# Attention values, projections and window scores in full 128x128 products, in a two-layer hybrid trunk on one core

## The chip, the cores and the metric

The kernel runs on 1 core of one Trainium2 chip. The metric is the device time of one execution in microseconds (us); three runs of the kernel before are known, and one profiled execution of it. Engines are named as in the profile: PE (TensorE matmul), PEld (its weight loads), DVE (VectorE), ACT (ScalarE), POOL (GpSimd), SP (the queue that issues the loads).

## The reference, cut to what matters

512 latent tokens and 256 context tokens, 1024 features, go through two layers. A layer is: half a SwiGLU, a mixer with four parallel parts, half a SwiGLU. In the last layer only the 512 latent tokens are wanted of the mixer's output. The part of the mixer that the change touches is the two attentions:

```python
q_a = mla_q(z_lat[0], g_mla_q, w_mla_uq, tab)      # 4 heads, 64 plain + 32 rotary
k_a, v_a = mla_kv(z_lat[1], z_lat[2], g_mla_kv, w_mla_ukv, tab)
o_a = dense_attend_blocked(q_a, concat(k_a, kc_a), concat(v_a, vc_a))   # latent queries: 768 keys
o_c = window_attend_latent(q, k, v, k_ctx, v_ctx, sink)  # 4 query heads, 2 key heads, 64 wide
# softmax in both; context queries attend to the 256 context tokens only
```

The query latent has 192 features (128 + 64), the key and value latent 128.

## The kernel before, in words

All activations lie with features on partitions and tokens along the free dimension. Every float32 operand is split into two parts of 12 bits, x = hi + lo (`split`, lines 128 to 134: ACT copies hi, DVE subtracts to get lo), and a product is three passes on PE (`mm3`, L162): lo\*hi, hi\*lo, hi\*hi; a pass over 768 tokens is two instructions, of 512 and 256 columns. The instruction order on each engine is fixed at build time by a scheduler that goes by program order, with `rise(n)` for work to be taken n instructions earlier.

`mixer(l, n, st)` runs once a layer, with n = 768 tokens in the first layer and 512 in the second (nq = 6 or 4 blocks of 128). It makes the modulated norm `x` (16 tiles), the input projection tile by tile (`proj`), the key and value latent `mkv`, the query latent `mqa` (128 rows) and `mqb` (its other 64 rows, split into two tiles; the 64 rows below are free), the window's `wq`, `wk`, `wv`, and the short convolution. Then comes attention, as a pipeline over units:

- `Latent(h, tp)`: 256 queries of a head; 4 heads by 3 or 2 units. `softmax` makes scores (three passes of 96 rows, L162), a maximum (L852), the exponential (L855) and a normalisation on POOL (L857).
- `Window(t, kv)`: 128 queries, one key head, two query heads (`g`). `softmax` makes the scores of the local blocks (L793), adds a mask by a product (L796), and the scores of the context blocks (L798). Each score is two passes: one with a head's hi and lo part stacked to 128 rows, one with hi alone, 64 rows.
- `turned` transposes the weights in blocks of 128 (L595) and splits them; `values` multiplies them with V in the one PSUM bank `po` (the tile `pone`): `mm3` with 64 columns of V's hi or lo part as the loaded operand and 256 columns of transposed softmax weights moving, three instructions for each key block. One ACT copy takes the result out: L879 (latent), L832 (window).

In step i the loop emits the scores of unit i, the transposes of unit i-1 and the values of unit i-2. `first_head` runs inside the short convolution, before the last of its column tiles (`pb`): weights, head 0, and the scores of unit 0. `mla_head` makes a head: `mla_rotary` for each pair of heads (64 columns), 64 columns of plain queries, 64 columns of keys; heads 1 to 3 are made at steps 1, 4, 7 (first layer) or 1, 3, 5 (second). `mla_query` is six passes: three with the 128 rows of `mqa`, three with the 64 rows of `mqb`. PSUM pieces: two double banks `dbls` (scores, projections), and two single banks `sgl` (transposes, V), which take the place of a third double bank once `pb` has been read.

Of the kernel before, what the change touches and what calls it, by code (L numbers as in the profile page):

```python
# [46 lines left out]
class K:  # L47
# [4 lines left out]
    LAGS, HEAD = (1, 2), 1  # L52
# [4 lines left out]
    def __init__(self, tc, ctx, a, out):  # L57
# [7 lines left out]
        # PSUM: two banks, and six that each phase cuts for itself  # L65
# [8 lines left out]
    # ---- buffers: handed out and given back in program order  # L74
# [5 lines left out]
    def area(self, name, side="left"):  # L80
        """A phase's buffers: each in a pool of its own, so that it waits only for the users of its own bytes."""
# [37 lines left out]
    def rise(self, n):  # L119
        """Work that the scheduler is to take as if it came n instructions earlier."""  # L120
# [6 lines left out]
    # ---- exact two-part split: x = hi + lo, each of 12 significant bits  # L127
# [13 lines left out]
    def unit(self, src, neg=False):  # L141
        """A split [parts, <= 512] block of weights."""
# [12 lines left out]
    def mm3(self, ps, w, x, start, stop):  # L155
        """ps += w^T x for split operands, each [K, M] / [K, N]; N is cut at PSUM's banks."""
# [49 lines left out]
    def need(self, l, part):  # L206
        """Has what is left of a part of the modulation computed."""
# [7 lines left out]
    def norm_gain(self, l, part, ks=(0, 4)):  # L215
        """g * (1 + scale), both conditions."""
# [32 lines left out]
    def sums(self, ps, tiles, n):  # L249
        """The sum over partitions and tiles, on all partitions."""  # L250
# [6 lines left out]
    def rsqrt(self, out, x, scale):  # L257
        """1 / sqrt(scale * x + eps)"""
# [3 lines left out]
    def spread(self, ps, rc):  # L262
        """A row of values by token on all partitions, from columns of values by token."""
# [3 lines left out]
    def inv_rms(self, ps, tiles, n, scale, j0=0):  # L267
        """1 / sqrt(scale * sum of squares + eps) on all partitions (in PSUM), found by token."""
# [9 lines left out]
    def rnorm(self, a, b, ps=None):  # L278
        """1 / rms(h) for tokens [a, b), on all partitions (in PSUM)."""
# [3 lines left out]
    def modulated(self, hi, lo, t, k, r, gain, l, part, a, b):  # L283
        """hi + lo = h[k] * gain * r + shift for tokens [a, b)."""
# [25 lines left out]
    def token_sums(self, X, hn):  # L310
        """T1 = B12 - B11, T2 = B22 - T1, T3 = B22 - B12, T4 = T2 - B21, split."""
# [24 lines left out]
    def half_load(self, idx, rs, f, m, kk):  # L336
        """Half of the features of the gate's (m = 0) or the up product's (m = 1) column tile f."""
# [8 lines left out]
    def whole(self, ps, w, x, hn, start, stop):  # L346
        """ps += a whole product over half of the features."""
# [4 lines left out]
    def hidden(self, g, j, hn, pss):  # L352
        """silu(gate) * up, split, for half j of the tokens."""
# [8 lines left out]
    def plain(self, idx, f, X, g, hn, fills):  # L362
        """The split hidden tile f by plain products."""
# [11 lines left out]
    def first_pairs(self, idx, X, g, hn, norm, operands, fills, start):  # L375
        """The first four hidden tiles by plain products, while the operands are being made."""
# [47 lines left out]
    def gate_up(self, idx, f, X, g, hn, fills):  # L424
        """g[0], g[1]: the split hidden tiles f and f + 1."""
# [192 lines left out]
    def mixer(self, l, n, st):  # L618
# [353 lines left out]
        for i in range(2):  # L972
# [9 lines left out]
            if i == 1:  # L982
                first_head()
# [306 lines left out]
```

## Time and profile before

| what | value |
|---|---|
| median of 3 runs | 2734.28 us (2730.88 to 2735.37) |
| span of the profiled execution | 2729.7 us, 41155 instructions |
| PE busy | 2687.2 us, 98% (16292 matmuls) |
| PEld busy | 2458.7 us, 90% |
| DVE busy | 1998.7 us, 73% |
| ACT busy | 1108.8 us, 41% |
| POOL busy | 65.5 us, 2% |
| mean granted TensorE clock | 0.995 |

The span runs from the first to the last instruction; of the profiled execution no other time is given, and its span lies 4.6 us below the median of the runs. A matmul's time in the profile reaches from its start to the end of its passage, so that neighbours overlap: what one costs in a stream is the distance from its start to the next one's start.

### The profile page before, as it was taken

The page shows a single profiled execution, that of the slowest core. Times are in us where ns is not written, and L with a number is a line of the kernel's source. Part 1 is how long each engine was busy: PE and PEld are TensorE (multiplying, and loading weights), DVE is VectorE, ACT ScalarE, POOL GpSimd, SP SyncE. Part 2 cuts the span into 40 slices and gives each one's busy share as a digit, 9 for nine tenths or more (in the row PEclk, how much of TensorE's full clock was granted, in tenths as well). Part 3 has the DMA queues.
Part 4 walks back from the last instruction along what each step waited for, and adds up shares of the span by engine and source line. Part 5 has one row for each costly group of instructions (what it writes and reads, how often), then busy time and mean ns, then how long its engine had stood idle before and what let it go on. Part 6 is the DMA issues. An engine that isn't in the chain of part 4 may idle for free.

```text
span 2729.7 us, 41155 instructions
## 1 busy us (share of the span) xinstructions
PE 2687.2 (98%) x16292; PEld 2458.7 (90%) x16292; DVE 1998.7 (73%) x3884; ACT 1108.8 (41%) x2096; POOL 65.5 (2%) x88
## 2 busy tenths in 40 slices
PE   7999999999999999999999999999999999999998
PEld 5999999988876899999999999999998877899998
DVE  5777666779785476767667867776678785698887
ACT  4333323343375342333234523343244375444444
POOL 0000000000022000000000000000000021000000
PEclk9999999999999999999999999999999999999999
DMA  7323222321123342323223132222222122423322
GB/s 269 108 101 100 79 96 90 108 83 57 55 78 93 109 139 93 101 93 103 83 85 124 48 100 70 63 79 60 63 85 99 58 78 78 138 94 98 104 93 78
DMA packets 78241, 254.83 MB, mean 93 GB/s; under 512 B 8672, under 2 KB 14048, under 8 KB 77792
## 3 DMA queue, kind: packets, MB, share of 16 engines
q1 hardware_dynamic: 78048, 252.21, 28.7%
q8 instruction: 127, 2.08, 0.3%
q14 instruction: 66, 0.54, 0.1%
HBM read 250.08 MB, written 2.10 MB: 92 GB/s over the span
## 4 chain that ended last, share of the span: by engine, by line
PE 94%; DVE 4%; DMA 1%; ACT 1%; issue 1%; POOL 0%; DVEq 0%; SPq 0%; POOLq 0%; ACTq 0%
PE ps L162 73%; PE pone L162 10%; PE pmod L179 3%; PE pmod L162 3%; PE ps L595 1%; PE ps L793 1%; PE ps L798 1%; DVE r L134 0%; DMA raw<-in_w_gu 0%; DVE sm L852 0%; PE ps L796 0%; DMA mraw<-in_w_mod 0%; DVE wl L134 0%; PE ps L272 0%; PE pone L272 0%
## 5 line engine op out<-in xcount | busy, mean ns | idle before, releaser
L162 PE MATMUL ps<-x,wh 128*128 128x384 f32 (+1 forms) x3064 | 748.9, 329 | 0.0
L162 PEld LDWEIGHTS ps<-x,wh 128*128 128x128 f32 x3064 | 542.7, 188 | 0.1
L162 PE MATMUL ps<-x,wl 128*128 128x384 f32 (+1 forms) x1532 | 506.1, 331 | 0.0
L133 ACT ACTIVATE wh<-raw 128x512 fp32r<-128x512 f32 (+1 forms) x445 | 278.3, 626 | 486.9 <-PE ps L162 336.3
L134 DVE TENSOR_TENSOR wl<-raw,wh 128x512 fp32r<-128x512 f32 (+1 forms) x445 | 305.2, 687 | 121.9 <-ACT wh L133 119.1
L162 PE MATMUL ps<-t,wh 128*128 128x384 f32 (+2 forms) x1488 | 385.2, 341 | 0.3 <-DVE t L134 0.3
L162 PE MATMUL ps<-r,wh 128*128 128x512 f32 (+7 forms) x1432 | 355.5, 350 | 0.3 <-DVE r L291 0.3
L296 DVE SCALAR_TENSOR_TENSOR h<-ps,hg,h 128x256 f32<-128x256 f32 (+3 forms) x404 | 186.8, 506 | 186.6 <-PE ps L162 186.1
L162 PEld LDWEIGHTS ps<-x,wl 128*128 128x128 f32 x1532 | 287.6, 188 | 12.9 <-issue 10.7
L162 PEld LDWEIGHTS ps<-t,wh 128*128 128x128 f32 x1488 | 269.2, 188 | 7.2 <-DVE t L134 0.5
L133 ACT ACTIVATE wh<-t 128x512 fp32r<-128x512 f32 x217 | 136.0, 629 | 337.1 <-PE ps L162 201.9
L162 PEld LDWEIGHTS ps<-r,wh 128*128 128x128 f32 (+3 forms) x1432 | 236.4, 184 | 36.1 <-DVE r L291 1.5
L450 DVE TENSOR_TENSOR t<-t,ps 128x384 f32<-128x384 f32 (+1 forms) x422 | 217.2, 520 | 52.6 <-PE ps L162 50.2
L162 PE MATMUL ps<-t,wl 128*128 128x384 f32 (+2 forms) x744 | 253.4, 342 | 1.6 <-ACT t L133 1.6
L162 PE MATMUL ps<-r,wl 128*128 128x512 f32 (+5 forms) x716 | 225.1, 355 | 2.4 <-ACT r L290 1.3
L134 DVE TENSOR_TENSOR wl<-t,wh 128x512 fp32r<-128x512 f32 x217 | 149.1, 689 | 95.2 <-ACT wh L133 95.0
L133 ACT ACTIVATE t<-t 128x384 fp32r<-128x384 f32 (+2 forms) x247 | 130.2, 536 | 208.9 <-DVE t L444 100.7
L162 PE MATMUL ps<-x,t 128*128 128x384 f32 (+1 forms) x1308 | 204.4, 310 | 0.0
L162 PEld LDWEIGHTS ps<-x,t 128*128 128x128 f32 x1308 | 194.4, 188 | 0.0
L162 PE MATMUL ps<-t,t 128*128 128x384 f32 (+2 forms) x948 | 188.9, 345 | 0.0
L162 PEld LDWEIGHTS ps<-t,t 128*128 128x128 f32 x948 | 165.5, 188 | 10.9 <-issue 1.2
L134 DVE TENSOR_TENSOR t<-t,t 128x384 fp32r<-128x384 f32 (+2 forms) x247 | 137.4, 568 | 25.4 <-ACT t L133 25.0
(215 smaller groups left out, 3711.0 us busy)
## 6 DMA issues: line engine op xcount, KB each, us to landing
raw<-in_w_gu SPq DMA_DIRECT2D x160, 512.0 KB, 3.8
mraw<-in_w_mod SPq DMA_DIRECT2D x128, 512.0 KB, 4.0
raw<-in_w_dn SPq DMA_DIRECT2D x88, 512.0 KB, 3.7
raw<-in_w_in SPq DMA_DIRECT2D x34, 512.0 KB, 3.3
raw<-in_w_out SPq DMA_DIRECT2D x20, 512.0 KB, 3.4
i<-in_w_mod SPq DMA_DIRECT2D x32, 256.0 KB, 6.0
raw<-in_w_gu SPq DMA_DIRECT2D x32, 256.0 KB, 3.5
h<-in_h SPq DMA_DIRECT2D x4, 768.0 KB, 6.6
```

What stands on the lines that cost most here:

```text
L133: self.nc.scalar.activation(hi, x, AF.Copy)
L134: self.nc.vector.tensor_tensor(out=lo, in0=x, in1=hi.bitcast(F32), op=ALU.subtract)
L162: self.nc.tensor.matmul(ps[:, c:e], a, b[:, c:e], start=start and i == 0, stop=stop and i == 2)
L179: nc.tensor.matmul(ps[32 * j:32 * j + 32, :256], self.sc[:, k, :], r[:, j * 256:(j + 1) * 256], start=k == 0, stop=k == KD - 1)
L296: nc.vector.scalar_tensor_tensor(out=self.h[:, k, s:e], in0=ps[:, s - a:e - a], scalar=gate[:, k, i:i + 1], in1=self.h[:, k, s:e], op0=ALU ...
L450: eng.tensor_tensor(out=out, in0=p, in1=q, op=op)
L595: self.nc.tensor.transpose(out, in_, self.ident)
L793: nc.tensor.matmul(ps[:, c0:SEQ], a, b[:, kc], start=i == 0, stop=False)
L798: nc.tensor.matmul(ps[:, SEQ:TOK], a, b[:, SEQ:], start=i == 0, stop=i == 1)
```

## The change

- V's hi and lo parts of a head lie side by side in 128 columns (`value_blocks`); `weigh` multiplies them with the lo and then the hi part of the weights, two instructions for each key block; the result's two halves of 64 rows are summed by an ACT copy and a DVE addition (`summed`).
- Queries and keys of the latent attention are projected for two heads at a time (128 columns): `mla_queries`, `mla_keys`; the rotary parts of all four heads at once (`mla_rotary`). `mqb` is one tile with hi in the lower and lo in the upper 64 rows; its weights (`query_weights`) are stacked both ways, so that the second part of `mla_query` is two passes of 128 rows in place of three of 64.
- Both passes of the window's scores have 128 rows (`wks` holds two stacked tiles for each key head).
- Order: only the queries of heads 0 and 1 are made before `pb`; their keys, the V tiles and the scores of unit 0 come after it; the pair 2, 3 is made at step 4 (first layer) or 2 (second).

```diff
-    LAGS, HEAD = (1, 2), 1
+    LAGS, PAIR = (1, 2), {3: 4, 2: 2}
...
+        def value_blocks(ts, src):
+            for j, t in enumerate(ts):
+                v = t.rearrange("p (q c d) -> p q c d", c=2, d=64)
+                self.split(v[:, :, 0, :], v[:, :, 1, :], src[:, j * 384:(j + 1) * 384].rearrange("p (q d) -> p q d", d=64))
+        def weigh(t, b, p, start, stop):
+            v = t[:, b * P:(b + 1) * P]
+            nc.tensor.matmul(po[:, :256], v, p[1], start=start, stop=False)
+            nc.tensor.matmul(po[:, :256], v, p[0], start=False, stop=stop)
+        def summed(out, c, w):
+            nc.scalar.activation(out, po[64:, c:c + w], AF.Copy)
+            nc.vector.tensor_tensor(out=out, in0=po[:64, c:c + w], in1=out, op=ALU.add)
...
-                    parts = (q[:, ts_], wks[1 + kv]), (q[rows, ts_], wks[0][rows])
+                    parts = (q[:, ts_], wks[kv][0]), (q[:, ts_], wks[kv][1])
...
-                    self.mm3(po[:64], (wvs[0][:, d], wvs[1][:, d]), p, j == 0, j == len(w.kts) - 1)
+                    weigh(wvs[kt // 3], kt % 3 * 2 + w.kv, p, j == 0, j == len(w.kts) - 1)
...
-                    nc.scalar.activation(oc[w.kv][...], po[:64, g * P:(g + 1) * P], AF.Copy)
+                    summed(oc[w.kv][...], g * P, P)
...
-                    self.mm3(po[:64], (vh[:, d], vl[:, d]), p, kt == k0, kt == 5)
+                    weigh(vt[b // 6], b % 6, p, kt == k0, kt == 5)
...
+        def mla_query(ps, c, wa, wb):
+            self.mm3(ps, (wa[0][:, c:c + P], wa[1][:, c:c + P]), (mqa[0][:, :n], mqa[1][:, :n]), True, False)
+            for i, w in enumerate(wb):
+                for a in range(0, n, 512):
+                    e = min(n, a + 512)
+                    nc.tensor.matmul(ps[:, a:e], w[:, c:c + P], mqb[:, a:e], start=False, stop=i == 1)
+        def mla_rotary(wa, wb):
+            ps, q = self.turn(self.dbl), self.S()
+            mla_query(ps[:, :n], 256, wa, wb)
+            nc.scalar.activation(q[:, :n], ps[:, :n], AF.Copy)
+            self.rope(q, 0, P, self.cos_m, self.sin_m, self.mask_m)
+            rot.extend(self.split_new(q[:, :n], n))
...
+        def mla_keys(h, w):
+            ps = self.turn(self.dbl)
+            self.mm3(ps, (w[0][:, h * 64:h * 64 + P], w[1][:, h * 64:h * 64 + P]), mkv, True, True)
+            for u in range(2):
+                kh, kl = ks[h + u] = self.R(), self.R()
+                self.split(kh[:64, :], kl[:64, :], ps[u * 64:u * 64 + 64, :TOK])
...
         def mla_values(w):
+            vt.extend(self.R() for _ in range(4))
+            for i in range(2):
+                ps = self.turn(dbls)
...
-            if i == 1:
-                first_head()
+            if i == 1:
+                first_queries()
...
+        self.dbl = dbls
+        kw = kv_weights()
+        mla_keys(0, kw)
+        self.give(qb)
+        mla_values(kw)
+        units[0].softmax()
+        qw = query_weights()
```

## Rows read from the trace of the kernel before

**Rows 1.** The page's first part: busy time, share, instructions

```profile
PE 2687.2 (98%) x16292; PEld 2458.7 (90%) x16292; DVE 1998.7 (73%) x3884; ACT 1108.8 (41%) x2096; POOL 65.5 (2%) x88
```

**Rows 2.** Stretches of attention: length; busy PE, PEld, DVE, ACT, POOL; clock; DMA

```profile
740.00:820.00 80.00, 75.57 (x517) 57.45 (x516) 65.98 (x132) 58.75 (x109) 18.26 (x21) 1.00 0.25 80
820.00:900.00 80.00, 78.91 (x518) 53.39 (x515) 47.66 (x121) 44.97 (x126) 17.50 (x28) 1.00 0.31 93
2180.00:2240.00 60.00, 57.12 (x358) 42.45 (x356) 54.78 (x103) 46.07 (x86) 13.41 (x12) 1.00 0.24 82
2240.00:2300.00 60.00, 59.76 (x375) 42.95 (x375) 35.35 (x79) 33.34 (x84) 12.61 (x17) 0.97 0.21 62
```

**Rows 3.** The same view, slices of 20 us

```profile
680.00:700.00 20.00, 20.00 (x117) 17.48 (x116) 20.00 (x39) 5.26 (x8) 0.00 (x0) 1.00 0.10 34
...
2180.00:2200.00 20.00, 18.38 (x106) 13.28 (x104) 19.05 (x35) 14.97 (x29) 2.50 (x2) 1.00 0.47 162
```

**Rows 4.** Timeline of PE, first head: start, length of the merged group, xcount

```profile
730.06 0.86 PE L162 MATMUL ps<-r,wh 128*128 128x512 f32 x4
730.76 0.51 PE L162 MATMUL ps<-r,wl 128*64 128x512 f32 x2
731.12 0.87 PE L162 MATMUL ps<-r,wh 128*64 128x512 f32 x4
731.91 0.56 PE L162 MATMUL ps<-r,wl 64*64 64x512 f32 x2
732.31 0.85 PE L162 MATMUL ps<-r,wh 64*64 64x512 f32 x4
733.09 0.56 PE L162 MATMUL ps<-r,wl 128*64 128x512 f32 x2
```

**Rows 5.** Timeline of PE, the V tiles

```profile
749.74 0.38 PE L162 MATMUL ps<-wh,r 128*128 128x256 f32 x1 [1.72 <-DVE f L985]
...
750.08 0.40 PE L162 MATMUL ps<-wh,r 128*128 128x256 f32 x2
750.32 0.28 PE L162 MATMUL ps<-wl,r 128*128 128x256 f32 x1
```

**Rows 6.** Timeline of PE, values and a transpose

```profile
763.03 0.88 PE L162 MATMUL pone<-f,r 128*64 128x256 f32 x6
...
763.74 0.29 PE L595 MATMUL ps<-ident,f 128*128 128x128 f32 x1
```

**Rows 7.** Timeline of PE, the scores of a window unit

```profile
862.80 0.69 PE L793 MATMUL ps<-r,r 128*128 128x256 f32 x2
863.42 0.33 PE L796 MATMUL ps<-masks_r,ident_r 128*128 128x128 f32 x1
863.59 0.64 PE L798 MATMUL ps<-r,r 128*128 128x256 f32 x2
864.16 0.69 PE L793 MATMUL ps<-r,r 128*128 128x256 f32 x2
```

**Rows 8.** Groups by line and shape, PE: xcount, busy us, mean ns

```profile
L162 PE MATMUL pone<-f,r 128*64 128x256 f32 x552 | 94.6, 296 | 0.8 <-DVE f L134 0.7
...
L798 PE MATMUL ps<-r,r 64*128 64x256 f32 x40 | 15.2, 381 | 0.0
...
L793 PE MATMUL ps<-r,r 64*128 64x384 f32 x16 | 7.0, 439 | 0.0
...
L793 PE MATMUL ps<-r,r 64*128 64x256 f32 x16 | 6.1, 381 | 0.0
```

**Rows 9.** Groups by line and shape, DVE, 740 to 906 us

```profile
L852 DVE TENSOR_REDUCE sm<-ps 128x1 f32<-128x768 f32 x16 | 15.1, 953 | 1.5 <-PE ps L162 1.2
...
L809 DVE TENSOR_TENSOR sm<-sm,vec 128x2 f32<-128x2 f32 x12 | 2.8, 230 | 0.7
L134 DVE TENSOR_TENSOR r<-ps,r 128x256 fp32r<-128x256 f32 x6 | 2.3, 421 | 1.1 <-ACT r L133 0.9
```

**Rows 10.** The same view, ACT

```profile
L879 ACT ACTIVATE f<-pone 64x256 f32<-64x256 f32 x12 | 4.5, 376 | 5.8 <-PE pone L162 5.8
```

More of the change, by code (lines that the diff above doesn't have):

```diff
@@ L708, in mixer @@
         mqa = self.split_new(qa[:, :n], n)
-        mqb = self.R(), self.R()
-        self.split(mqb[0][:64, :n], mqb[1][:64, :n], qb[:64, :n])
+        mqb = self.R()
+        lower, upper = slice(0, 64), slice(64, P)
+        nc.scalar.activation(mqb[lower, :n], qb[lower, :n], AF.Copy)
+        nc.vector.tensor_tensor(out=mqb[upper, :n], in0=qb[lower, :n], in1=mqb[lower, :n].bitcast(F32), op=ALU.subtract)
         self.give(qa)
@@ L782, in softmax @@
                 t, kv, b0, b1, c0 = w.t, w.kv, w.b0, w.b1, w.c0
-                rows, ts_ = slice(kv * 64, kv * 64 + 64), slice(t * P, (t + 1) * P)
+                ts_ = slice(t * P, (t + 1) * P)
                 mx, sm, es = self.sm_t(2), self.sm_t(2), self.sm_t(2)
@@ L917, in mla_weights @@
-        def mla_weights():
-            return (self.unit(self.load(self.a["w_uqa"][l], 384)[:, :384]), self.unit(self.load(self.a["w_uqb"][l], 384, 64)[:64, :384]),
-                    self.unit(self.load(self.a["w_ukv"][l], 512)[:, :512]))
-        def mla_values(w):
-            vt.extend((self.R(), self.R()) for _ in range(2))
-            for t in range(6):
-                ps = self.turn(sgl)
-                s = slice(t * P, (t + 1) * P)
-                d = slice((t % 3) * 256, (t % 3) * 256 + 256)
-                self.mm3(ps[:, :256], (mkv[0][:, s], mkv[1][:, s]), (w[0][:, 256:512], w[1][:, 256:512]), True, True)
-                self.split(vt[t // 3][0][:, d], vt[t // 3][1][:, d], ps[:, :256])
+                summed(oa[m.h // 2][(m.h % 2) * 64:(m.h % 2) * 64 + 64, m.tp * 256:(m.tp + 1) * 256], 0, 256)
@@ new lines, in mla_keys @@
+        def mla_keys(h, w):
+            ps = self.turn(self.dbl)
+            self.mm3(ps, (w[0][:, h * 64:h * 64 + P], w[1][:, h * 64:h * 64 + P]), mkv, True, True)
+            for u in range(2):
+                kh, kl = ks[h + u] = self.R(), self.R()
+                self.split(kh[:64, :], kl[:64, :], ps[u * 64:u * 64 + 64, :TOK])
+                if h == 0:
+                    self.split(kh[64:96, :], kl[64:96, :], qb[64:96, :])
+                else:
+                    nc.scalar.activation(kh[64:96, :], ks[1][0][64:96, :].bitcast(F32), AF.Copy)
+                    nc.vector.tensor_copy(kl[64:96, :], ks[1][1][64:96, :].bitcast(F32))
+                heads[h + u] = qs[h + u], ks[h + u]
@@ new lines, in query_weights @@
+        def query_weights():
+            wa = self.unit(self.load(self.a["w_uqa"][l], 384)[:, :384])
+            r = self.turn(self.raw)
+            for s in (lower, upper):
+                nc.sync.dma_start(r[s, :384], self.a["w_uqb"][l])
+            ul, lu = (t[:, :384] for t in self.turn(self.wr))
+            with self.rise(self.P_UNIT):
+                nc.scalar.activation(ul[lower], r[lower, :384], AF.Copy)
+                nc.scalar.activation(lu[upper], r[upper, :384], AF.Copy)
+                for s, hi, lo in ((lower, ul, lu), (upper, lu, ul)):
+                    nc.vector.tensor_tensor(out=lo[s], in0=r[s, :384], in1=hi[s].bitcast(F32), op=ALU.subtract)
+            return wa, (lu, ul)
@@ new lines, in kv_weights @@
+        def kv_weights():
+            return self.unit(self.load(self.a["w_ukv"][l], 512)[:, :512])
+        def mla_values(w):
+            vt.extend(self.R() for _ in range(4))
+            for i in range(2):
+                ps = self.turn(dbls)
+                for t in range(3):
+                    s = slice((3 * i + t) * P, (3 * i + t + 1) * P)
+                    self.mm3(ps[:, t * 256:(t + 1) * 256], (mkv[0][:, s], mkv[1][:, s]), (w[0][:, 256:512], w[1][:, 256:512]), True, True)
+                value_blocks(vt[2 * i:2 * i + 2], ps)
@@ L965, in mixer, with first_queries @@
         ob = []
-        def first_head():
-            mw = mla_weights()
-            mla_head(0, *mw)
-            units[0].softmax()
+        def first_queries():
+            qw = query_weights()
+            mla_rotary(*qw)
+            mla_queries(0, *qw)
         for i in range(2):
@@ L997, in mixer @@
         for i in range(len(units) + lv):
-            if i and i % per == self.HEAD % per and len(heads) < 4 and i >= self.HEAD:
-                mla_head(len(heads), *mw)
-                if len(heads) == 2:
-                    self.give(qb)
-                if len(heads) == 4:
-                    self.give(*mkv, *mqa, *mqb)
+            if i == self.PAIR[per]:
+                mla_queries(2, *qw)
+                self.give(*mqa, mqb, *rot)
+                mla_keys(2, kw)
+                self.give(*mkv)
             if 0 < i < len(units):
@@ L1019, in mixer @@
             if i == nl - 1 + lv:
-                for hi, lo in vt:
-                    self.give(hi, lo)
+                self.give(*vt)
                 for j, t in zip((0, 1), oa):
@@ L1031, in mixer @@
             self.give(*qs)
-        self.give(*wks, *wvs)
+        self.give(*(t for w in wks for t in w), *wvs)
         return o
```

68 lines of the change are left out of this document (20 added, 48 removed).

## The prediction

> **What bounds the kernel now.** I read the page first: PE is busy for 98% of the span [rows 1], so work taken from PE should come out of the time unless another engine takes its place. But a matmul's shown time overlaps its neighbours', so this share hides small gaps, and the change touches two short stretches only. Therefore I read busy times by stretch next. The attention of the first layer fills about 740 to 900 us, that of the second 2180 to 2300; in both the first part is latent attention, the second the window [rows 2]. PE is busy there for 271 of 280 us, but DVE, 73% over the span, has 66.0 of 80 and 54.8 of 60 us in the two latent parts, and 47.7 of 80 and 35.4 of 60 in the window parts [rows 2]. So there are two engines to watch: PE sets the time now, and DVE stands close behind it. Third, the timelines give what a matmul costs in a stream, from start to start; the groups by shape give the counts.
>
> **PE: columns that fall away.** Pitches first. Two passes over 768 tokens, four instructions of 512, 256, 512, 256 columns, start at 730.06 and the next group at 730.76: 0.70 us, so 0.35 us a pass of 768 [rows 4]. A 256-column matmul with 64 loaded columns takes 0.71/6 = 0.118 us (763.03 to 763.74) [rows 6]; with 128 loaded columns 0.24/2 = 0.12 (750.08 to 750.32) [rows 5]. So the wider load of the new value product stays covered, and one instruction costs what it cost. A 512-column instruction is then 0.35 - 0.118 = 0.232 us.
>
> - Values: three instructions for each key block become two. There are 552 now [rows 8], so 184 go: 184 x 0.118 = 21.7 us.
> - Queries: a layer has two rotary products and four heads, of six passes each: 36. Afterwards it has one rotary product and two pairs, of five passes: 15. The 21 passes cost 0.35 us in the first layer and 0.232 in the second (512 tokens): 21 x 0.582 = 12.2 us.
> - Keys: 12 passes of 768 become 6 in each layer: 12 x 0.35 = 4.2 us.
>
> Together 38.1 us. The V projection, the transposes, the masks and the latent scores keep their matmuls; the second window pass keeps its columns and gets twice the rows.
>
> **PE: changes of the row count.** In a window unit two 256-column score passes, the second of 64 rows, take 0.62 us until the mask starts (862.80 to 863.42), and the two over the context 0.57 (863.59 to 864.16) [rows 7]; without a change they would take 0.236 each. The 64-row passes thus cost 0.38 + 0.33 = 0.72 us a query head beyond their columns, about 0.18 for each change into or out of them. The groups of 64 rows are 16 + 16 for the local blocks and 40 for the context [rows 8]: 32 pairs of groups x 0.72, and 8 context groups that stand alone x 0.34, make 25.8 us. In the queries, the four instructions ahead of a change take 0.79 and 0.78 us in place of 0.70 [rows 4]: 0.17 for each of six products in each layer, 2.1 us. All of it goes, as every row count around them becomes 128: 27.9 us. If a row change cost nothing by itself and the delay were only a late operand, this term would be 0; I take the rows, as the delay stands in the local and the context passes alike, with no wait shown.
>
> The Trainium skill, page "TensorEngine Tiling (Array Packing)", section "Key Properties", says that changing the tiling mode drains the engine. For 64 rows the trace agrees, with the 0.18 us above. By the page's list of configurations 128x64 is a mode of its own too, so that the values (64 columns) beside transposes (128 columns) would drain as well; there the trace does not agree: six values and the step to a transpose keep 0.118 us a piece [rows 6].
>
> PE work removed: 38.1 + 27.9 = 66.0 us, of which 36.4 in the first layer (values 11.8, queries 7.4, keys 2.1, row changes 15.1) and 29.4 in the second.
>
> **DVE: what is added.** Each unit's result now needs a DVE addition from PSUM behind the ACT copy: 20 latent units of 64x256, 40 halves of window units of 64x128. The nearest rows are 0.42 us for 256 columns and 0.23 for two columns [rows 9]; I take 0.42 and, between the ends, 0.30. First layer: 12 x 0.42 + 24 x 0.30 = 12.2; second: 8 x 0.42 + 16 x 0.30 = 8.2 us. By number the rest about cancels: four operations of one rotary embedding and a split go, two key copies, two window-key splits and the stacked weights' second half come. ACT gains some small copies and has 21 and 14 us free in the latent parts [rows 2]. The added half of the query weights' load is one more issue on SP for each set, but one set of key weights is no longer loaded twice; DMA is a quarter busy there [rows 2].
>
> **What DVE allows.** DVE's work in the two stretches becomes 65.98 + 47.66 + 12.2 = 125.8 us, where PE would like to be done in 160 - 36.4 = 123.6; and 54.78 + 35.35 + 8.2 = 98.3 us, where PE asks for 120 - 29.4 = 90.6. So DVE becomes the bound. How full can it be? The fullest attention slice has 19.05 of 20, 0.95 [rows 3]; just ahead of attention it reaches 20.00, with independent work queued [rows 3]; the latent part of the first layer holds 0.82 [rows 2], but there PE was the limit. I take 0.95, for the bounds 1.00 and 0.90. At 0.95 the stretches last 132.4 and 103.5 us: 8.8 and 12.9 us longer than PE asks. At 1.00: 2.2 and 7.7. At 0.90: 16.2 and 18.6. So DVE takes back 22 us of the 66, between 10 and 35.
>
> **The start of attention.** Before, the scores of unit 0 lay beside the `pb` product; PE waited once, 1.72 us at the first V product, for the PSUM that `pb` had used [rows 5]. Now keys, their splits, V and unit 0's scores stand behind `pb`, and PE has the V products to run meanwhile (18 x 0.12 = 2.2 us). The old wait should go, as V no longer uses these banks. Against it, some five DVE operations of up to 0.95 us (splits of two heads, one maximum) [rows 9] lie bare: from a gain of 1.7 to a loss of 4.8 - 2.2 + a second maximum 0.95 = 3.6 us a layer. I take a loss of 1.5 a layer, 3 us.
>
> **Sum.** 66 - 22 - 3 = 41 us. Span 2729.7 - 41 = 2688.7 us; the runs' median stands 4.6 us above that span, so I put the time at 2734.3 - 41 = 2693 us, 1.5% faster. With both DVE bounds and both start bounds the gain lies between 66 - 35 - 7 = 24 and 66 - 10 + 3 = 59: 2675 to 2710 us.
>
> **The rivals.**
>
> - *PE stays the bound.* Splits for later use (the output weights, the window's operands) may leave the attention stretch, so that DVE has room: the whole 66 us, 2668 us. For it speaks that DVE has 40% free in the window parts [rows 2]; against it, that the sum over both parts leaves none.
> - *DVE and PE wait for each other.* Each unit goes from scores over DVE, ACT and POOL to transposes, splits and values. If DVE gets no fuller than the 0.82 that it shows in the first latent part [rows 2], the stretches take 153 and 120 us: a gain of 7 us, 2727 us. For it speaks that this chain is as long as before, with one more link; against it, that PE and not the chain set the pace at 0.82.
> - *Slower: the one bank of the values.* `pone` comes free only when the DVE addition is done, not after the 0.38 us ACT copy [rows 10]. If in each of 40 units the addition stood behind two reductions or splits of 0.95 us [rows 9] and PE behind it, that is 40 x 2.3 = 92 us against 66: 26 us slower, 2760 us. It decides from 66/40 = 1.65 us a unit. Against it: between one unit's values and the next stand the scores of another unit, over 1 us of PE work [rows 7].
> - *64-column products drained too.* By the skill's reading above, the values' change between 64 and 128 columns would be saved as well. Cut in three by transposes, 40 units have up to 240 changes; at 0.18 us this is 43 us more off PE, and if DVE does not bind, 2734 - 109 = 2625 us. [rows 6] speak against it.
> - *The change does nothing that counts:* DVE gives PE's whole gain back, 2734 us.
>
> **Chances.** My forecast's range (a gain of 24 to 59) 0.58; PE the bound (59 to 70) 0.13; mutual waiting (a gain of 6 to 24) 0.15; columns drained too 0.02; within 0.2% 0.05; slower 0.07. A difference of 0.2%, 5.5 us, is about what a measurement of this kernel can tell from no change. Faster: 0.58 + 0.13 + 0.15 + 0.02 = 0.88. For 8 in 10 the range takes in PE as the bound and the nearer half of mutual waiting: 2668 to 2717 us.
>
> **What would show it.** Right: `pone` has 368 matmuls of 128x128 at a pitch near 0.12; no score product of 64 rows is left, and two score passes of 256 columns take 0.24 us to the next start; attention lasts some 28 us less in the first layer and 16 in the second; DVE is at 0.9 or more there and PE's waits name DVE splits or maxima. Wrong: PE waits for DVE additions on `pone` in most units (slower rival); DVE stays near 0.8 with PE waiting; 128-column loads stretch the value pitch beyond 0.12; or the order of instructions moves and the gain lies outside attention.

## The result, and the profile after

The changed kernel takes 2717.68 us (median of 4 runs, 2714.86 to 2723.23), the one before 2734.82 us beside it (4 runs, 2730.88 to 2735.85): 0.994 of the time, 95% interval 0.9927 to 0.9953. It is faster, by 17 us where 41 were forecast, and its time lies 0.7 us above the range that the prediction gave for 8 in 10 (2668 to 2717 us). The profiled executions differ by 2729.7 - 2714.5 = 15.2 us.

The first part of its page, for [rows 1]:

```profile
PE 2640.3 (97%) x16021; PEld 2443.1 (90%) x16021; DVE 2014.1 (74%) x3940; ACT 1116.9 (41%) x2098; POOL 66.0 (2%) x88
```

PE's busy time fell by 47 us and DVE's rose by 15; the span did not follow PE. First the pieces. The two lines of `weigh` over the whole run (columns: xcount, then least, median and largest ns, first and last start, shapes):

```profile
L765 PE MATMUL pone<-f,r x184: 277/282/562, 769.1 to 2306.9; 128*128 128x256 f32 x184
```
```profile
L766 PE MATMUL pone<-f,r x184: 274/281/562, 769.3 to 2307.0; 128*128 128x256 f32 x184
```

The timeline of PE, a window unit's scores and the values behind them, for [rows 6, 7]:

```profile
830.79 0.51 PE L812 MATMUL ps<-r,r 128*128 128x256 f32 x2
831.14 0.22 PE L815 MATMUL ps<-masks_r,ident_r 128*128 128x128 f32 x1
831.20 0.45 PE L817 MATMUL ps<-r,r 128*128 128x256 f32 x2
831.48 0.29 PE L765 MATMUL pone<-f,r 128*128 128x256 f32 x1
831.61 0.28 PE L766 MATMUL pone<-f,r 128*128 128x256 f32 x1
831.72 0.28 PE L765 MATMUL pone<-f,r 128*128 128x256 f32 x1
831.84 0.28 PE L766 MATMUL pone<-f,r 128*128 128x256 f32 x1
...
862.50 0.39 PE L812 MATMUL ps<-r,r 128*128 128x256 f32 x2
862.73 0.22 PE L815 MATMUL ps<-masks_r,ident_r 128*128 128x128 f32 x1
```

There are 368 `pone` matmuls, 0.12 us apart (831.48 to 831.84 in three steps). The two local score passes take 0.35 us to the next start and the context's two 0.28, for 0.62 and 0.57 before; at 862.50, behind score passes of the same shape, the local two take 0.23, against a forecast of 0.24. DVE's additions, 740 to 906 us (columns as in [rows 9]):

```profile
L770 DVE TENSOR_TENSOR f<-pone,f 64x128 f32<-64x128 f32 x24 | 6.7, 280 | 2.3 <-ACT f L769 1.6
...
L770 DVE TENSOR_TENSOR f<-pone,f 64x256 f32<-64x256 f32 x12 | 5.0, 414 | 0.4 <-ACT f L769 0.2
```

So the pieces have about their forecast sizes. The count of matmuls is exact: 16292 - 16021 = 271 fewer, which are 184 of the values, 63 of the queries and 24 of the keys. Now the stretches, between the same pieces of work in both kernels: a latent part from the start of DVE's product on `pb` to the first window maximum, a window part from there to the last one. Columns as in [rows 2]; of each kernel the first layer's two parts, then the second's. Before:

```profile
748.70:827.50 78.80, 75.37 (x528) 56.87 (x528) 62.07 (x131) 58.35 (x114) 19.74 (x23) 1.00 0.26 81
827.50:893.80 66.30, 65.22 (x413) 42.86 (x414) 39.73 (x101) 36.48 (x102) 14.76 (x23) 1.00 0.28 86
2189.30:2249.30 60.00, 57.07 (x372) 43.34 (x367) 52.38 (x101) 46.04 (x88) 16.28 (x15) 1.00 0.22 74
2249.30:2301.70 52.40, 52.40 (x321) 36.22 (x321) 29.95 (x70) 27.45 (x72) 9.97 (x14) 0.97 0.22 63
```

After:

```profile
745.30:829.20 83.90, 71.27 (x457) 56.45 (x457) 69.33 (x144) 61.43 (x114) 19.02 (x23) 0.88 0.28 88
829.20:887.00 57.80, 51.20 (x385) 37.39 (x387) 42.74 (x120) 36.05 (x101) 14.83 (x21) 0.97 0.39 128
2176.40:2245.00 68.60, 56.97 (x341) 45.82 (x341) 59.13 (x112) 51.17 (x90) 16.23 (x15) 0.85 0.24 72
2245.00:2289.90 44.90, 40.57 (x317) 30.28 (x315) 32.42 (x84) 27.39 (x71) 11.26 (x16) 1.00 0.43 138
```

The window parts are 8.5 and 7.5 us shorter, the latent parts 5.1 and 8.6 us longer: together only 2.3 us. The other 12.9 us lie outside: `pb` comes 3.4 us sooner, the way from the last maximum to the second layer's `pb` is 6.1 us shorter, the end 3.4. Some of this is work that moved. The products that make the modulation (`pmod`, L179) do not hang on attention and are spread over most of the kernel; 339 of them fall into the four parts where 263 did (35.1 us busy for 29.3), and the stretches behind attention have 77 fewer (5.8 us). With as many as before the four parts would, by this count, be some 8 us shorter and not 2.3. In the four parts PE is busy for 220.0 us, 30.0 less than before, but it now stands idle for 35.2 us (255.2 - 220.0) where it stood 7.4. DVE holds 0.79 of the first layer's two parts and 0.81 of the second's, before 0.70 and 0.73; it is 0.83 and 0.86 in the latent parts and 0.74 and 0.72 in the window parts. And the granted clock, 1.00 in both latent parts before, is 0.88 and 0.85.

Where PE waits, 735 to 915 us, the five largest totals (total, times, longest):

```profile
PE ps L162 <- DVE r L134: 5.4, 2, 3.4
PE pone L765 <- DVE f L770: 2.3, 2, 2.0
PE ps L162 <- ACT f L873: 2.1, 4, 0.7
PE pmod L179 <- DMA mraw<-in_w_mod: 2.0, 1, 2.0
PE ps L595 <- POOL f L833: 1.9, 4, 0.7
```

No one engine is named: DVE, ACT, POOL and a transfer all are. Only at the start is there one long wait, in the timeline of PE:

```profile
746.33 0.39 PE L162 MATMUL ps<-wh,r 128*128 128x256 f32 x1 [1.22 <-DVE f L1018]
...
751.08 0.58 PE L162 MATMUL ps<-wh,r 128*128 128x256 f32 x1 [3.42 <-DVE r L134]
...
755.15 1.41 PE L162 MATMUL ps<-r,r 96*128 96x512 f32 x6
```

and of DVE there:

```profile
747.36 0.95 DVE L134 TENSOR_TENSOR r<-ps,r 64x768 fp32r<-64x768 f32 x1
748.23 1.81 DVE L134 TENSOR_TENSOR r<-f,r 128x768 fp32r<-128x768 f32 x2
750.07 1.55 DVE L134 TENSOR_TENSOR r<-ps,r 64x768 fp32r<-64x768 f32 x2
...
756.60 0.96 DVE L870 TENSOR_REDUCE sm<-ps 128x1 f32<-128x768 f32 x1
```

V's second half needs a double bank that the two heads' keys still hold; the second key's split stands on DVE behind two splits for something else. V, and then unit 0's scores, come late: the first maximum starts 11.3 us after DVE's product on `pb`, and 11.7 in the second layer. In the kernel before it started 3.3 and 1.8 us ahead of that product.

### The profile page after: what moved, and what is told of

It reads as the page before. It is cut to its first block, busy times and chain, and to the rows that moved or that the text cites. A ratio compares the mean times of both kernels' runs of the same rounds, so it can differ in the third digit from the quotient of the medians.

```text
span 2714.5 us, 40707 instructions
## 1 busy us (share of the span) xinstructions
PE 2640.3 (97%) x16021; PEld 2443.1 (90%) x16021; DVE 2014.1 (74%) x3940; ACT 1116.9 (41%) x2098; POOL 66.0 (2%) x88
## 4 chain that ended last, share of the span: by engine, by line
PE 91%; DVE 4%; ACT 3%; DMA 1%; issue 1%; POOL 0%; DVEq 0%; SPq 0%; ACTq 0%; POOLq 0%
PE ps L162 74%; PE pone L162 8%; PE pmod L162 3%; PE pmod L179 3%; PE ps L595 1%; DMA mraw<-in_w_mod 1%; PE pone L765 1%; PE pone L766 1%; ACT f L826 1%; DMA raw<-in_w_gu 0%; ACT f L133 0%; DVE r L134 0%; ACT f L873 0%; POOL f L833 0%; PE pone L272 0%
## 5 line engine op out<-in xcount | busy, mean ns | idle before, releaser
L133 ACT ACTIVATE wh<-raw 128x512 fp32r<-128x512 f32 x439 | 274.8, 627 | 464.6 <-PE ps L162 313.9
L134 DVE TENSOR_TENSOR wl<-raw,wh 128x512 fp32r<-128x512 f32 x439 | 301.6, 688 | 104.9 <-ACT wh L133 102.5
L162 PE MATMUL ps<-r,wh 128*128 128x512 f32 (+3 forms) x1362 | 338.0, 350 | 0.3 <-DVE r L291 0.3
L162 PEld LDWEIGHTS ps<-x,wl 128*128 128x128 f32 x1532 | 287.8, 188 | 12.9 <-issue 10.7
L162 PEld LDWEIGHTS ps<-r,wh 128*128 128x128 f32 (+1 forms) x1362 | 228.0, 188 | 31.8 <-DVE r L291 1.5
L162 PE MATMUL ps<-r,wl 128*128 128x512 f32 (+4 forms) x681 | 212.2, 352 | 1.3 <-ACT r L290 1.3
```

What stands on the lines that cost most here:

```text
L133: self.nc.scalar.activation(hi, x, AF.Copy)
L134: self.nc.vector.tensor_tensor(out=lo, in0=x, in1=hi.bitcast(F32), op=ALU.subtract)
L162: self.nc.tensor.matmul(ps[:, c:e], a, b[:, c:e], start=start and i == 0, stop=stop and i == 2)
```

## Experiments

Four theories share the missing 24 us. *Start:* V in the double banks holds up keys and scores. *Fill:* DVE has too much to do, and less work on DVE, above all the additions, gives time back. *Clock:* the half clock slows PE. *Chain:* with less work on PE a unit's own way through scores, maximum (DVE), exponential (ACT), POOL, transposes, splits and values sets the period, with every engine below full. The experiments ran in five groups, each on one chip with the kernel before beside it: e1 to e4, e5 to e8, e9 to e12, e13 to e16, e17 and e18. That kernel's medians go from 2731.1 to 2737.1 us over the groups. So a difference of some 6 us between groups says little, and where one is named both readings stand: by the medians, and by the gain of each over the kernel before beside it (its own gain).

| run | us, median (range) | before beside it | ratio, 95% |
|---|---|---|---|
| e1_window_rows | 2713.09 (2712.82 to 2713.80) | 2731.09 | 0.9930 (0.9913 to 0.9946) |
| e2_window_values | 2714.98 (2713.65 to 2718.33) | 2731.09 | 0.9938 (0.9924 to 0.9953) |
| e3_no_additions | 2712.37 (2710.06 to 2713.86) | 2731.09 | 0.9926 (0.9911 to 0.9941) |
| e4_v_own_banks | 2706.51 (2705.78 to 2707.97) | 2731.09 | 0.9906 (0.9891 to 0.9921) |
| e5_rows_and_pairs | 2711.25 (2710.52 to 2714.18) | 2737.06 | 0.9915 (0.9899 to 0.9931) |
| e6_scores_first | 2706.78 (2703.77 to 2711.51) | 2737.06 | 0.9898 (0.9879 to 0.9918) |
| e7_subtract_on_pool | 2713.71 (2711.26 to 2716.27) | 2737.06 | 0.9922 (0.9906 to 0.9939) |
| e8_dummy_products | 2714.68 (2707.02 to 2720.00) | 2737.06 | 0.9932 (0.9907 to 0.9958) |
| e9_first_and_pool | 2705.75 (2704.10 to 2712.14) | 2734.03 | 0.9897 (0.9881 to 0.9913) |
| e10_four_buffers | 2710.48 (2705.94 to 2715.19) | 2734.03 | 0.9910 (0.9891 to 0.9930) |
| e11_no_values_first | 2709.36 (2706.82 to 2710.36) | 2734.03 | 0.9905 (0.9890 to 0.9920) |
| e12_no_values_pool | 2707.86 (2705.68 to 2712.53) | 2734.03 | 0.9903 (0.9887 to 0.9920) |
| e13_first_no_max | 2682.20 (2679.34 to 2683.10) | 2731.61 | 0.9810 (0.9795 to 0.9826) |
| e14_before_no_max | 2720.81 (2720.21 to 2722.32) | 2731.61 | 0.9954 (0.9937 to 0.9971) |
| e15_no_values_no_max | 2693.53 (2689.74 to 2696.68) | 2731.61 | 0.9853 (0.9836 to 0.9870) |
| e16_first_no_additions | 2703.11 (2701.09 to 2705.20) | 2731.61 | 0.9889 (0.9874 to 0.9904) |
| e17_dummies_throughout | 2716.14 (2713.52 to 2716.99) | 2735.81 | 0.9928 (0.9915 to 0.9942) |
| e18_first_dummies | 2711.48 (2703.44 to 2711.62) | 2735.81 | 0.9906 (0.9892 to 0.9920) |

Three came out slower than any theory had said beforehand: e5, e10 and e11.

**Parts alone: e1, e2.** e1 is the kernel before with 128-row window scores and nothing else; e2 adds V side by side, with the heads and their order as before.

```diff
-                    parts = (q[:, ts_], wks[1 + kv]), (q[rows, ts_], wks[0][rows])
+                    parts = (q[:, ts_], wks[kv][0]), (q[:, ts_], wks[kv][1])
```

> The kernel before with 128 rows in both window score passes and nothing else of the change. PE loses the 25.8 us that the row changes cost. Theory A (the gain is lost where attention starts, in the new order of keys, V and scores): the start is as before, so most of it shows, 2709 to 2716 us. Theory B (DVE's work over the whole of attention takes the gain back): little DVE work is added (some 4 us), so it shows here too. If the row changes had no price of their own: 2733 to 2737 us.

> The kernel before with the window's 128 rows and V's two parts side by side, DVE additions included; heads are made one by one and start beside the short convolution, as before. PE loses 25.8 + 21.7 = 47.5 us. Theory A: the start is not touched, so 2690 to 2702 us, faster than the changed kernel, which also has the projections in pairs. Theory B: the additions are all in, DVE stays full, 2712 to 2722 us.

The rows alone give 18.0 us, as much as the whole change. e1's stretches:

```profile
750.40:830.30 79.90, 77.14 (x535) 57.85 (x535) 64.30 (x135) 59.88 (x117) 20.78 (x23) 1.00 0.27 80
830.30:884.10 53.80, 51.73 (x406) 39.34 (x407) 37.96 (x101) 36.05 (x101) 15.28 (x22) 1.00 0.35 103
2180.80:2241.70 60.90, 58.66 (x390) 44.41 (x383) 54.60 (x108) 48.21 (x91) 16.13 (x15) 1.00 0.20 65
2241.70:2282.00 40.30, 40.18 (x308) 31.93 (x308) 28.17 (x66) 26.10 (x70) 9.88 (x14) 1.00 0.30 91
```

The window parts lose 12.5 and 12.1 us: 24.6, for the 25.8 forecast. Some 6.5 us of it come back in small pieces around them (`pb` 1.7 us later, the latent parts 1.1 and 0.9 longer, the rest behind the window parts); why is open. PE's busy time falls by 18.8 us (2687.2 to 2668.4) with the same number of matmuls, so the row changes cost between 19 and 25 us. The window parts of the changed kernel, with fewer matmuls for the values, are 4.0 and 4.6 us *longer* than these; 1.5 and 2.3 us of that is PE time of `pmod` products that moved in. e2 is no faster than e1: a third of the value products taken from PE gave nothing.

**Start: e4, e6.** e4 puts V into the two single banks, in four groups of 384 columns; e6 also emits unit 0's scores ahead of V.

```diff
-            for i in range(2):
-                ps = self.turn(dbls)
...
+            for j in range(4):
+                ps = self.turn(sgl)
...
-        mla_values(kw)
         units[0].softmax()
+        mla_values(kw)
```

> The changed kernel with the V products in the two single banks (four groups of 384 columns) in place of the two double banks that keys and scores use. Theory A: V no longer waits for the key splits, and unit 0's scores no longer for V's splits; the wait of 3.4 us in the first layer goes and with it some time at half clock: 2705 to 2714 us. Theory B: nothing, 2715 to 2721 us.

> The changed kernel with V in the single banks and the scores of unit 0 ahead of the V products in program order. Theory A: unit 0 starts some 3 us earlier in each layer and V fills PE meanwhile, 2698 to 2706 us (V in its own banks alone gave 2706.5). Theory B: the units' period stays, 2704 to 2709 us.

e4 takes 11.2 us less than the changed kernel by the medians, and 7.4 by own gain (24.6 for 17.1). The traces agree: the first maximum follows `pb`'s product by 7.6 and 8.1 us, for 11.3 and 11.7, which makes 7.3 us. So of the missing time 7 to 11 us are the start's. In e6 the first maximum follows by 5.7 and 6.7 us; by the medians e6 takes as long as e4, by own gain (30.3) it is 5.7 us better. The rest is still there in e6, whose first latent part has the full clock and lasts 77.1 us:

```profile
744.60:821.70 77.10, 65.50 (x462) 50.12 (x462) 69.50 (x145) 61.00 (x114) 21.09 (x23) 1.00 0.30 96
821.70:878.90 57.20, 50.79 (x385) 37.44 (x387) 42.49 (x119) 35.95 (x100) 14.84 (x21) 0.97 0.39 130
2168.00:2232.60 64.60, 53.80 (x360) 42.69 (x359) 58.79 (x112) 50.61 (x90) 16.40 (x15) 0.95 0.27 85
2232.60:2278.40 45.80, 41.50 (x325) 30.62 (x323) 32.24 (x85) 27.46 (x71) 11.79 (x16) 1.00 0.45 146
```

PE has 11.6 us idle in the first of these and 6.4 in the second, DVE 7.6 and 14.7. So with the start mended DVE does reach 0.90 and 0.91 in the latent parts; in the window parts it stays at 0.74 and 0.70, and PE stands idle in both.

**Fill: e3, e16, e7, e9, e12.** e3 is the changed kernel, e16 e6, without DVE's addition: the second half of the value product stays out of the result. e7, e9 and e12 put the subtractions of the window's operands and the rotary copies on POOL, in the changed kernel, in e6 and in e11.

```diff
             nc.scalar.activation(out, po[64:, c:c + w], AF.Copy)
-            nc.vector.tensor_tensor(out=out, in0=po[:64, c:c + w], in1=out, op=ALU.add)
```
```diff
-                    nc.vector.tensor_tensor(out=t[b, :n], in0=q[a, :n], in1=t[a, :n].bitcast(F32), op=ALU.subtract)
+                    nc.gpsimd.tensor_tensor(out=t[b, :n], in0=q[a, :n], in1=t[a, :n].bitcast(F32), op=ALU.subtract)
```

> The changed kernel without the DVE additions behind the values: only the upper half of each result is copied out, so the hi part's product is left out of the output. Theory A: 2711 to 2717 us, since the additions lie behind the start. Theory B: DVE loses about 17 us of work and the bank of the values comes free earlier, 2697 to 2705 us.

> The run with V in the single banks and unit 0's scores first, without the DVE additions (only the upper half of each result is copied out, so the output lacks the hi part's product). Theory B2: the chain from a unit's values to the next is shorter by one link and DVE has 20 us less, 2697 to 2703 us against 2706.8. If the additions were free: 2705 to 2708 us.

> The changed kernel with the subtractions that make the window's operands and the copies of the rotary lo parts on POOL in place of DVE: some 13 us of DVE work less in each layer. If DVE's amount of work bounds the latent part (theory B1): 2700 to 2708 us. If the length of the chain does (theory B2), or the start (theory A): within 4 us of the changed kernel, 2714 to 2721, or slower where POOL's normalisation stands behind them.

> The run with V in the single banks and unit 0's scores first, with the window operands' subtractions and the rotary copies on POOL as well. In that run DVE's durations fill the latent parts (71.5 of 71.4 us, 58.2 of 57.9). Theory B1 (the amount of DVE work bounds the latent parts): they fall to about 64 and 52 us, the time to 2693 to 2698 us. Theory B2 (the chain through buffers and engines): the latent parts stay within 2 us, 2703 to 2709 us.

> As the one before, with the window operands' subtractions and the rotary copies on POOL. Theory B1: 6 us or more below the one before, 2692 to 2699 us, since DVE's work in the latent parts falls by 10 us. Theory B2: within 3 us of the one before.

Without the additions DVE is busy for 17.6 us less in e3 (1996.5 for 2014.1), which is 5.3 us faster than the changed kernel by the medians and 1.6 with each against its own kernel before. e7 relieves DVE of 9.9 us and gains 4.0, or 6.2. With the start mended, 16.2 us less bring 3.7 (e16 beside e6), 11.3 us bring 1.0 (e9 beside e6) and 15.5 us bring 1.5 (e12 beside e11). The first two pairs are from different groups, and by own gain e16 and e9 are 1.8 and 2.0 us *behind* e6; e12 and e11 are from one group. All of it is near or within the runs' scatter: at most 0.1 to 0.2 us for each us taken from DVE. e7, e9 and e12 have a second cost, as POOL does the work of the units' normalisation too: for its result in the latent units (L875, L876) PE waits 4.2 us in e7's two attentions for none in the changed kernel's, and 5.6 in e12's for 1.0 in e11's, so these runs understate what DVE's relief is worth. e16 has no such cost. In e12 the latent parts last 75.8 and 63.0 us for 77.4 and 63.3 in e11, although DVE's work in them falls from 64.8 to 56.7 and from 56.4 to 50.4 us. DVE's amount alone is not the bound.

**Clock: e8, e17, e18.** Products of 128x512 into `po` that nobody reads keep PE at work: e8 30 a layer around the start of the changed kernel; e17 49 in the first layer and 37 in the second, through the latent parts; e18 the same in e6.

```diff
+        def warm(k, a=kw[0], b=mkv[0]):
+            for _ in range(k):
+                nc.tensor.matmul(po, a[:, :P], b[:, :512], start=True, stop=True)
...
+                if 0 < i < nl:
+                    warm(3, vt[0], vt[0])
```

> The changed kernel with 30 products of 128x512 whose result is thrown away (the bank of the values, before its first use) in each layer, where PE waits at the start of attention: 7 us of PE work at full clock put into gaps. Theory C (the gaps lower the granted clock, and the products at half clock cost more than the gaps): the granted clock stays 1.00 up to the first units and the time falls, 2707 to 2714 us. Theory A without the clock: the products only fill waits, 2716 to 2722 us, or up to 2730 where they delay work.

> The changed kernel with 49 products of 128x512 that nobody reads in the first layer's latent part and 37 in the second's (16 at the start of attention, three at each later latent step), some 20 us of PE work in PE's idle time. Executions of one kernel differ by about 0.72 us for each us of lost clock (1 minus the granted clock, times the span): e6 took 2703.8 and 2704.0 at 0.993, 2709.5 and 2711.5 at 0.990. Theory that the half clock is the bulk of what is missing: the clock returns to 0.994 or more, and of the 2717.7 us some 0.72 x 20 = 14 go: 2700 to 2708 us. Theory that the units' chain over DVE, ACT and POOL sets the period and the half clock lies mostly beside it: whatever the clock, 2712 to 2722 us.

> The same idle products in the version with V in single banks and scores first (e6, 2706.8 us, clock 0.990 to 0.993). Theory of the clock: 0.994 or more, 2698 to 2704 us. Theory of the chain: 2705 to 2713 us, as the extra products stand ahead of some of the units' own.

e8's executions spread over 13 us and settle nothing; the other two do. The stretches of e18:

```profile
743.70:821.30 77.60, 72.52 (x499) 57.82 (x498) 70.02 (x143) 60.19 (x112) 19.89 (x23) 1.00 0.29 96
821.30:878.50 57.20, 51.18 (x400) 36.99 (x401) 43.43 (x120) 36.83 (x103) 14.83 (x21) 1.00 0.41 130
2167.50:2233.40 65.90, 59.56 (x388) 48.45 (x386) 60.71 (x112) 49.89 (x89) 16.32 (x15) 0.97 0.25 81
2233.40:2277.20 43.80, 40.87 (x320) 29.85 (x317) 32.16 (x86) 28.33 (x73) 11.73 (x15) 1.00 0.42 134
```

and of e17:

```profile
745.00:826.40 81.40, 73.75 (x494) 57.13 (x493) 69.39 (x144) 60.50 (x112) 18.92 (x23) 1.00 0.29 91
826.40:883.90 57.50, 51.56 (x400) 37.38 (x401) 43.38 (x121) 36.99 (x103) 14.83 (x21) 1.00 0.42 129
2171.30:2242.60 71.30, 61.77 (x380) 48.98 (x379) 59.71 (x112) 49.86 (x88) 15.14 (x15) 0.93 0.25 82
2242.60:2288.30 45.70, 42.21 (x338) 31.34 (x336) 33.41 (x86) 28.82 (x74) 11.85 (x15) 1.00 0.44 139
```

In e18 86 products more, some 20 us (86 x 0.232), leave the first latent part at 77.6 us for 77.1 and all four parts at 244.5 for 244.7: they are free there, so PE has that much room. In e17 the clock comes back (1.00 and 0.93 in the latent parts, 0.993 over the span in all five executions) and the four parts last 255.9 us for 255.2, the whole run 2716.14 for 2717.68. Since the clock returns and brings next to nothing, it was probably not the bound. That its gain and a delay by the extra products cancel is not excluded: the first latent part is 2.5 us shorter, the second 2.7 longer. The times of both kernels still follow the clock from one execution to the next (e18: 2703.44 us at 0.995, 2711.41 to 2711.62 at 0.992 and 0.993); in which stretch those executions lost it, no trace shows.

**Values: e5, e11.** e5 is the changed kernel with the old value products (rows and pairs alone); e11 is e5 with scores first and the keys raised.

```diff
-                    weigh(vt[b // 6], b % 6, p, kt == k0, kt == 5)
+                    self.mm3(po[:64], (vh[:, d], vl[:, d]), p, kt == k0, kt == 5)
```

> The changed kernel with V's values as before (three products with 64 loaded columns, no DVE additions, V in the single banks): the window's 128 rows and the projections in pairs alone. PE loses 25.8 + 18.5 us. Theory A (start of attention): V no longer shares the double banks, so a part of the start comes back: 2700 to 2708 us. Theory B (the chain from scores over DVE, ACT and POOL to values gives a unit a period that PE can't shorten, and the additions lengthen it): the window part falls to that of the run with the window's rows alone (54 and 40 us in place of 58 and 45), 2700 to 2708 us too; the two differ in the stages: A shortens the time from the short convolution to the first latent maximum, B the window part.

> Window rows and pairs, V's products as in the kernel before; unit 0's scores ahead of V, its keys raised by 150 instructions. Theory A (start): the start falls from 7 to under 4 us in each layer, 2701 to 2707 us against 2711 for the same without the new order. Theory B (values are no gain, as the chain and not PE sets a unit's period): at or below the run with values in the same order, 2706.8 us.

Without V side by side the changed kernel is 6.4 us *faster* (8.7 by own gain). V's start is the old one too, and both theories came in part: the first maximum follows `pb`'s product by 6.6 and 7.6 us for 11.3 and 11.7, and the window parts last 54.1 and 41.4 us, as in e1, for 57.8 and 44.9. With the start mended on both sides, e9 stands 2.1 us ahead of e12 in one group, ranges overlapping, and e6 2.6 ahead of e11 (5.6 by own gain). The part that was to take 21.7 us off PE is worth some 2 us, at most 6.

**Chain: e13, e14, e15, e10.** e13 is e6 without the maxima, e14 the kernel before and e15 e11 without them: the exponential takes a constant small scale and no maximum, so its values are not the softmax. e10 gives e6 a fourth pair of buffers for the transposed weights.

```diff
-                    nc.vector.reduce_max(mx, ps[:, k0:TOK], axis=AX.X, negate=True)
-                    nc.vector.tensor_tensor(out=mx, in0=mx, in1=sc, op=ALU.mult)
...
-                    nc.scalar.activation(pr[:, k0:], ps[:, k0:TOK], AF.Exp, scale=sc, bias=mx, accum_out=sm)
+                    nc.scalar.activation(pr[:, k0:], ps[:, k0:TOK], AF.Exp, scale=1e-4, accum_out=sm)
```

> The run with V in the single banks and unit 0's scores first, without the maxima of the scores (and with a constant small scale in the exponentials, so that they stay finite): the softmax is flattened and the output is not the reference's. DVE loses 80 maxima, 61 us in all, and every unit's chain from scores to exponentials is about 1.1 us shorter. Theory B2 (a unit's chain over PE, DVE, ACT and POOL, not the amount of one engine's work, sets the stretch): PE becomes the bound again and most of the removed PE work shows, 2668 to 2685 us. If start and clock were all that is left: 2698 to 2706 us.

> The kernel before, without the maxima in the same way (the output is not the reference's). Theory B2: PE set the time of attention there, so little comes out, 2718 to 2730 us, and the distance to the same cut in the changed kernel with the repaired start is 40 us or more, where with the maxima it is 27. If DVE or the chain had bounded the kernel before as well: 2690 to 2710 us.

> Window rows and pairs without V side by side, unit 0's scores first, without the maxima (not the reference's output). Theory B2: with PE as the bound the values' 21.7 us count, so this is 12 to 22 us slower than the same with V side by side; with the maxima the two were equal (2706.8 and 2709.4). If the value products never were worth their PE time: equal again.

> The run with V in the single banks and unit 0's scores first, with four pairs of buffers for the transposed weights in place of three (the running sum of the norm, idle in the mixer, lends its place). Theory B2 (transposes wait until values have read a buffer, so that units move in step): the window parts fall by 3 us or more each, 2696 to 2703 us. Theory B1: no change, 2703 to 2709 us.

One link out of the chain, the one between scores and exponential, gives e13 24.6 us beside e6 (19.1 by own gain), and 10.8 in the kernel before. Then the change with its start mended is worth 38.6 us (2720.81 to 2682.20), where with the maxima it is worth 30.3 (e6, own gain), and V side by side 11.3 (2693.53 to 2682.20; e15 also has its keys raised). Both are just under the 40 and 12 us expected at least. In the four parts, taken by the exponentials in place of the maxima, the difference is plainer: 212.2 us in e13 for 247.2 in e14, 35.0 less, where e6 has 12.8 less than the kernel before. PE is idle there for 11.9 us, for 33.1 in e6, and in 740 to 900 us for 6 of 160:

```profile
740.00:820.00 80.00, 74.63 (x523) 59.56 (x522) 59.40 (x110) 65.05 (x133) 23.51 (x26) 0.98 0.31 94
820.00:900.00 80.00, 79.57 (x538) 58.99 (x536) 39.89 (x101) 48.23 (x122) 14.82 (x22) 1.00 0.37 109
```

So most of PE's saving was real, and it lay idle behind work on the other engines. That 38.6 us come near the 41 of the forecast confirms nothing, since the forecast had DVE take back 22 of 66: with DVE relieved, 63 should have shown, and some 24 of them still do not. e13 takes 60.9 us off DVE (2013.1 to 1952.2) and so less DVE work as well as a link. By the medians the additions, DVE work at the chain's end, gave 0.23 us for a us of DVE time, the subtractions off the chain 0.1, the maxima 0.40; by own gain the additions gave nothing and the maxima 0.31. That leans to the chain and does not show it: a share of the fill is not excluded. A fourth buffer pair gave nothing, so these buffers do not hold the chain alone. More score banks, or a longer lag between scores and values, were not tried.

## Why the prediction was too large

- **PE work removed, 66 us: right in its counts and pitches, in time perhaps a little large.** The 271 matmuls and the 0.12 us are as forecast. PE's busy time fell by 46.9 us; to this comes the clock's loss in the four parts (0.12 x 83.9 + 0.03 x 57.8 + 0.15 x 68.6 - 0.03 x 52.4 = 20.5 us), which makes at most 67, for a clock that is low while PE waits slows nothing. Between e14 and e13, whose clocks are alike (0.996 and 0.995), busy time falls by 52.5 us. The row changes, 25.8 us, cost 19 to 25 (e1). The rival of drained 64-column products is not borne out: e13 gains 11.3 us on e15 where the columns alone are 21.7. The Trainium skill's rule that a change of the tiling mode drains the engine (page "TensorEngine Tiling (Array Packing)", section "Key Properties") agrees with e1 for 64 rows; for 64 columns no run shows it.
- **DVE additions, 20.4 us: right in size** (0.28 and 0.41 us for 0.30 and 0.42), and cheap in time: without them the run gains 1.6 to 5.3 us (e3) or at most 3.7 (e16).
- **"What DVE allows", 0.95: this step failed.** I took the fullest slice of 20 us for what a whole stretch can hold, and one figure for latent and window parts together. Over the stretches DVE reached 0.79 and 0.81, under my lower bound of 0.90, with PE idle for 35.2 us in place of 7.4. With the start mended the latent parts do reach 0.90 (e6); the window parts, with less DVE work, stay at 0.74 and 0.70. Attention became 3.4 us shorter in the first layer and 1.1 longer in the second, where 28 and 16 less were to show; that the gain lies outside attention was one of my signs of being wrong. The rival "DVE and PE wait for each other", with its 0.82 and a gain of 6 to 24 us, came nearest; that 17 us lie in its range is in part luck, since it had the gain inside attention. My argument against it, that PE and not the chain had set the pace at 0.82, was true of the kernel before and no evidence for the one after: once PE has room the waits among the engines set the pace, at nearly the same number. Nor was DVE's amount of work the bound that the step made of it: less of it gave little (e9, e12, e16).
- **"The start of attention", a loss of 3 us: mis-sized.** Mending it in part gives back 7 to 11 us (e4). The step counted DVE's splits, but not the order on DVE nor that keys, V and scores pass through the same two double banks: 3.42 us of wait at one product.
- **Not foreseen: the granted clock.** In the latent parts it fell to 0.88 and 0.85; with PE's room it cost little or nothing that shows (e17).
- **Open:** which link of the chain binds, how much of the rest is DVE's fill, and why some 24 us do not show even without the maxima. Best of the versions with the full result are e9 (2705.75 us), e4 (2706.51) and e6 (2706.78), alike within their scatter: by the medians half of the way to the forecast.

## What to carry to other kernels

Where PE is 98% busy but its products hang in a chain over three other engines, a saving on PE can end in waits for those engines. Products nobody reads, added in a trial, tell whether PE has room by then, and a link taken out tells what that link and its work cost. The fullest short slice of an engine is no measure of what a stretch of dependent work can hold: take what such stretches show, each kind for itself (here DVE reached 0.9 in the latent parts and 0.74 in the window parts). When a stretch has room, work that runs beside it moves in, so count that work before comparing the stretch's length. Before work that passes through the same PSUM banks is put in a row, count who holds each bank and what stands ahead on DVE of the operation that frees it.

## What the runs showed of the hardware

In the changed kernel the granted clock was 0.52 from 786 to 790 us, near the lower of its two levels (1.2 of 2.4 GHz), and there a value product takes 0.21 us to the next start for 0.12 (timeline of PE):

```profile
788.28 0.41 PE L765 MATMUL pone<-f,r 128*128 128x256 f32 x1
788.49 0.41 PE L766 MATMUL pone<-f,r 128*128 128x256 f32 x1
788.71 0.41 PE L765 MATMUL pone<-f,r 128*128 128x256 f32 x1
788.92 0.41 PE L766 MATMUL pone<-f,r 128*128 128x256 f32 x1
```

In the 20 us from 740 and from 2180, where PE was busy for 14.3 and 16.0 us, it stood at 0.83 and 0.66.

A visit of the `pmod` products, which load 32 columns, costs about the same for two as for eight: in the kernel before 0.55 us from 765.19 to the next start at 765.74 for two, 0.57 from 756.57 to 757.14 for eight, with no wait shown. Taking them in larger groups was not tried.

POOL takes twice DVE's time for a subtraction of 64x768, 1.97 us in e7 for 0.95 on DVE in the changed kernel:

```profile
L973 POOL TENSOR_TENSOR r<-f,r 64x768 fp32r<-64x768 f32 x4 | 7.8, 1970 | 5.6 <-ACT r L972 4.1 <-issue 1.4
```
